# Taking the norm boundary into the feed-forward part: four up tiles, chunk by chunk

## The chip, the cores and the metric

The kernel runs on one core of a Trainium2 chip. The time is that of one execution on the device, in microseconds (us); the median of the runs counts, and lower is better. Engines: TensorE (PE; its weight loads are PEld), VectorE (DVE), ScalarE (ACT), GpSimd (POOL) and SyncE (SP), which issues transfers.

## The reference, cut to what matters

One inference step of a two-layer decoder. Each layer has a mixer (gated DeltaNet in the first, latent attention in the second) and a convolutional feed-forward part; each of the four is wrapped in two norms, and the sum is kept in x. Width 1024, feed-forward width 2816; 1040 prompt tokens and 8 sample tokens, 1048 in all. The change touches the place where the mixer's result is normed and added to x, x is normed for the feed-forward part, and its first up-projections begin.

```
def rmsnorm(x, w):
    xf = x.astype(jnp.float32)
    y = xf * lax.rsqrt(jnp.mean(xf * xf, axis=-1, keepdims=True) + NORM_EPS)
    return (y * w.astype(jnp.float32)).astype(x.dtype)

def conv_ffn(h, prev, w_up, conv_w, conv_b, w_down):
    u, new_prev = causal_dwconv(h @ w_up, prev, conv_w)
    gate, val = jnp.split(u + conv_b, 2, axis=-1)
    return (jax.nn.silu(gate) * val) @ w_down, new_prev

        x = x + rmsnorm(o, p['a_norm_post'][i])
...
        o, fconv = conv_ffn(rmsnorm(x, p['f_norm_pre'][layer]), ffn_conv0[layer],
                            p['f_w_up'][layer], p['f_conv_w'][layer], p['f_conv_b'][layer], p['f_w_down'][layer])
        x = x + rmsnorm(o, p['f_norm_post'][layer])
```

## The kernel before, in words

**Layout.** Features lie on the 128 partitions in 8 blocks, tokens along the free axis in three chunks (`CH`): chunk 0 with 280 tokens (the 8 samples, then 272 prompt tokens), chunks 1 and 2 with 384 each. The order of work is `ORD`, chunk 1, 2, 0. Every operand of a large product is split into a high half and the rest (`xh`, `xl` for activations, `wh`, `wl` for weights), and a product is three matmuls (`mm3`, L226 to L229): wh by xh (L227), wh by xl (L228), wl by xh (L229). A tile of up-projection over one chunk (`proj`) is 8 blocks of three, 24 matmuls.

**Weights.** `wprep` loads a 128-column tile, folds the norm's gain into it on GpSimd (L144), copies the high half on ScalarE (L151) and subtracts the low half on VectorE (L152).

**Output projection** (`outp`). It fills `acc` chunk by chunk in the order of `ORD`, 8 blocks each, through the two "mm" buffers of PSUM (`psop`); VectorE adds the result to `acc` (L336). In the first layer the last part of it has two heads (six matmuls for a block of a chunk), in the second layer four heads (twelve).

**Boundary** (`boundary`, one chunk). ScalarE squares `acc` in four pairs of blocks, VectorE adds them up (L259), two matmuls with ones make the statistic (`st_ps`, L265, issued at high priority; one row of a view counts each as two), ScalarE takes ln and exp (L106, L107). Then for each pair of blocks the old x is loaded (`xr`), `acc` is scaled (L285) and the residual added (L287, twice a pair). Then the high half on ScalarE (L293), its squares, their sum on VectorE (L259), the low half on GpSimd (L295), and a second statistic, whose result goes to `RS`. The up-projection reads `xh` and `xl` unscaled; `RS` is multiplied in when its result leaves PSUM.

**What calls it.** `boundaries` opens pools of its own, two statistic buffers in PSUM ("st") among them, runs the boundary for the three chunks, and closes them. Only then `ffn` opens its pools: the buffers for the products g (`fg`, four each of "gh" and "gl"), u and y (`fu`), down weights (`fdw`), and in PSUM "dn" (four) and "tr" (two).

**Feed-forward** (`ffn`). First six batches of stored convolution rows are loaded (`fsrow`, in the y buffers), transposed by TensorE into "tr" (`fpst`, L945, 44 transposes in all) and copied to `fstT` (L946). Then 11 groups of two pairs; a pair is one gate and one value tile, 24 matmuls for each chunk through the "mm" buffers. VectorE takes the result out of PSUM into `u` (L963, L964 for chunk 0, L966 for the others). `up_end` makes the convolution: ScalarE the first tap (L973), VectorE the other two (L975, over all 1064 columns, so all three chunks of the tile have to be there). Then silu, product (L999), high half and low half of g (L1004, L1007). The first pair alone goes chunk by chunk: both tiles on chunk 1, both on chunk 2, both on chunk 0. Every later tile takes its chunks in the order 0, 1, 2. From the second group on `down` of the group before comes in (`fdn`, in "dn").

**Order on the engines.** Nothing is put in order by hand at this place. A scheduler ranks the instructions by their order in the code and by buffers coming free, with the statistic's matmuls raised by `high_priority(2000)`, so each engine's order is not the order of the code.

## Time and profile before

| | us |
|---|---|
| median of 3 runs | 3313.66 |
| lowest, highest | 3309.49, 3319.81 |
| profiled execution | 3314.68 |
| its span | 3312.9 |

The mean granted clock of TensorE was 0.975 in the profiled execution. The part of it that the change touches lies at two places: from about 846 to 960 us (boundary of the first layer's mixer and the first up tiles) and from about 2455 to 2570 us (the same in the second layer). The views name instructions by line, engine and the program's names; "x4" counts instructions, and a number behind "<-" in brackets is idle time with what ended it. In the second layer the normed chunks have the names xbh and xbl, in the first xfh and xfl.

### The profile page before, as it was taken

The numbers are of one execution on the slowest core, as the hardware profiler recorded it, in microseconds if no ns is written. First come the engines' busy times: TensorE is split into PE (matmuls) and PEld (weight loads), VectorE is DVE, ScalarE is ACT, GpSimd is POOL, SyncE is SP. The second block draws the span as 40 slices with busy tenths as digits, with TensorE's granted clock in tenths as the row PEclk, the third lists the DMA queues.
The fourth block names the chain that finished last, engine by engine and source line by source line (L and its number), as shares of the span: only waits on it lengthen the run. The fifth ranks groups of instructions, "written<-read, shape, count | busy, mean of one in ns | idle before, by whom it ended". The sixth has DMA issues, their size and how long they took to land.

```text
span 3312.9 us, 52527 instructions
## 1 busy us (share of the span) xinstructions
PE 3123.5 (94%) x20846; PEld 2884.2 (87%) x20846; DVE 2030.3 (61%) x4139; ACT 1254.9 (38%) x2541; POOL 862.2 (26%) x1013
## 2 busy tenths in 40 slices
PE   7999999999899999999978999999998999999997
PEld 6888888888799999999967888856678999999996
DVE  4777777766864555555576676544557355555556
ACT  4656555563433222222334444433224322222223
POOL 1433222210342222322342111111105332322322
PEclk9999999999899999999989999999998999999999
DMA  3222222235321111111121000354432111111111
GB/s 107 62 65 69 64 67 59 72 105 176 96 66 46 39 52 49 48 46 39 45 86 44 25 27 28 108 189 184 159 102 84 46 46 45 46 45 52 46 39 66
DMA packets 267650, 235.08 MB, mean 71 GB/s; under 512 B 57919, under 2 KB 246597, under 8 KB 263285
## 3 DMA queue, kind: packets, MB, share of 16 engines
q1 hardware_dynamic: 260224, 189.69, 19.7%
q0 software_dynamic: 6912, 41.95, 3.4%
q8 instruction: 164, 2.69, 0.3%
q14 instruction: 82, 0.66, 0.1%
q10 hardware_dynamic: 268, 0.09, 0.0%
HBM read 198.84 MB, written 33.40 MB: 70 GB/s over the span
## 4 chain that ended last, share of the span: by engine, by line
PE 76%; DVE 14%; DMA 3%; issue 3%; ACT 2%; POOL 1%; SPq 0%; ACTq 0%; POOLq 0%; DVEq 0%
PE fps L228 9%; PE fps L229 9%; PE fps L227 9%; PE fdn L228 5%; PE fdn L227 5%; PE fdn L229 5%; PE psu L227 2%; PE psu L229 2%; PE po L1408 2%; PE psu L228 2%; PE dscr L1493 2%; DVE acc L287 2%; PE psop L227 1%; DVE tm L658 1%; DVE xs L660 1%
## 5 line engine op out<-in xcount | busy, mean ns | idle before, releaser
L144 POOL TENSOR_TENSOR ws<-ws,vec 128x1024 f32<-128x1024 f32 (+1 forms) x127 | 249.5, 1965 | 424.3 <-DMA ws<-in_f_w_up_dram 210.1
L228 PE MATMUL fps<-xfl,wh 128*128 128x384 f32 (+1 forms) x1056 | 343.7, 326 | 8.2 <-POOL xfl L295 8.1
L227 PE MATMUL fps<-xfh,wh 128*128 128x384 f32 (+1 forms) x1056 | 341.8, 324 | 8.0 <-ACT xfh L293 7.0
L228 PE MATMUL fps<-xbl,wh 128*128 128x384 f32 (+1 forms) x1056 | 343.6, 325 | 4.8 <-POOL xbl L295 4.7
L227 PE MATMUL fps<-xbh,wh 128*128 128x384 f32 (+1 forms) x1056 | 341.6, 324 | 1.1 <-ACT xbh L293 0.5
L229 PE MATMUL fps<-xfh,wl 128*128 128x384 f32 (+1 forms) x1056 | 342.4, 324 | 0.0
L229 PE MATMUL fps<-xbh,wl 128*128 128x384 f32 (+1 forms) x1056 | 341.2, 323 | 0.0
L966 DVE TENSOR_TENSOR fu<-fps,RS 128x384 f32<-128x384 f32 x176 | 98.0, 557 | 386.6 <-PE fps L229 386.1
L151 ACT CAST wh<-ws 128x1024 fp32r<-128x1024 f32 (+1 forms) x144 | 148.0, 1027 | 491.6 <-PE fps L228 373.8
L227 PE MATMUL fdn<-gh,dh 128*128 128x384 f32 (+1 forms) x960 | 315.2, 328 | 0.0
L228 PE MATMUL fdn<-gl,dh 128*128 128x384 f32 (+1 forms) x960 | 311.6, 325 | 0.0
L229 PE MATMUL fdn<-gh,dl 128*128 128x384 f32 (+1 forms) x960 | 308.6, 321 | 0.0
L1044 DVE TENSOR_TENSOR acc<-acc,fdn 128x384 f32<-128x384 f32 (+1 forms) x432 | 216.7, 514 | 108.8 <-PE fdn L229 108.0
L227 PE MATMUL psu<-xah,wh 128*128 128x384 f32 (+1 forms) x768 | 261.8, 341 | 9.5 <-ACT u L533 5.1
L228 PE MATMUL psu<-xal,wh 128*128 128x384 f32 (+1 forms) x768 | 260.0, 339 | 0.7 <-DVE xal L223 0.7
L229 PE MATMUL psu<-xah,wl 128*128 128x384 f32 (+1 forms) x768 | 259.0, 337 | 0.7 <-DVE wl L152 0.7
L975 DVE SCALAR_TENSOR_TENSOR fy<-fu,fcv,fy 128x1064 f32<-128x1064 f32 x176 | 238.6, 1357 | 7.6 <-ACT fy L973 7.3
L152 DVE TENSOR_TENSOR wl<-ws,wh 128x1024 fp32r<-128x1024 f32 (+1 forms) x144 | 173.6, 1206 | 71.3 <-ACT wh L151 71.1
L228 PEld LDWEIGHTS fps<-xfl,wh 128*128 128x128 f32 x1056 | 200.7, 190 | 10.8 <-POOL xfl L295 10.5
L227 PEld LDWEIGHTS fps<-xfh,wh 128*128 128x128 f32 x1056 | 200.3, 190 | 9.4 <-ACT xfh L293 7.9
L228 PEld LDWEIGHTS fps<-xbl,wh 128*128 128x128 f32 x1056 | 200.5, 190 | 6.9 <-POOL xbl L295 6.5
L227 PEld LDWEIGHTS fps<-xbh,wh 128*128 128x128 f32 x1056 | 200.2, 190 | 1.7 <-ACT xbh L293 0.9
(963 smaller groups left out, 7856.1 us busy)
## 6 DMA issues: line engine op xcount, KB each, us to landing
ws<-in_f_w_up_dram SPq DMA_DIRECT2D x88, 512.0 KB
ds<-in_f_w_down_dram SPq DMA_DIRECT2D x44, 512.0 KB
ws<-in_a_w_in_dram SPq DMA_DIRECT2D x32, 512.0 KB
xt<-in_x_prompt_dram SPq DMA_DIRECT2D x16, 512.0 KB
of<-og_d SPq DMA_DIRECT2D x32, 192.0 KB
xr<-x_d SPq DMA_DIRECT2D x16, 384.0 KB
GC<-gcd SPq DMA_DIRECT2D x24, 174.0 KB
Ss<-in_state_delta_S_dram SPq DMA_DIRECT2D x8, 512.0 KB
```

The costliest lines, as they stand in the source:

```text
L144: G.tensor_tensor(st, st, bc(fo, [P, kt, m]), op=ALU.mult)
L151: A.copy(hi, st)
L152: V.tensor_tensor(lo, st, hi, op=ALU.subtract)
L227: PE.matmul(ps, wh, ah, start=start, stop=False)
L228: PE.matmul(ps, wh, al, start=False, stop=False)
L229: PE.matmul(ps, wl, ah, start=False, stop=stop)
L287: V.scalar_tensor_tensor(a_[:, k + j, :], a_[:, k + j, :], vc(wname, k + j), res[j], op0=ALU.mult, op1=ALU.add)
L966: V.tensor_tensor(u[:, 18 + t0:18 + t0 + n], ps[:, :n], RS[:, t0:t0 + n], op=ALU.mult)
L975: V.scalar_tensor_tensor(y, u[:, j:j + LW], fcv[:, l, j, tl:tl + 1], y, op0=ALU.mult, op1=ALU.add)
L1044: V.tensor_tensor(acc[c][:, m, :], acc[c][:, m, :], ps[:, :n], op=ALU.add)
L1408: PE.matmul(po[:, :nq], vt[:kk, kb, P * (h % 2):P * (h % 2) + P], pT[:kk, j, :nq], start=(kb == 0), stop=(kb == i))
L1493: PE.matmul(sc[32 * j:32 * j + 32, :], ql[:, k, b, :], cT[:, j, :], start=(k == 0), stop=False, tile_position=(0, 32 * j))
```

## The change

`boundaries` is gone. `ffn` gets the name of the norm as an argument, and a new function `up_first` runs, for each chunk of `ORD`, its boundary and then four up tiles (the two pairs of the first group) on that chunk. What changes with it:

- The results of these four tiles go to the four "dn" buffers of PSUM (`up_mm(..., first=True)`), no longer to the two "mm" buffers.
- Gate and value tile of the second pair get their weight halves in the down weights' buffers ("dh", "dl") and their `u` in a "gh" and a "gl" buffer, which are made 1066 columns wide for that.
- The boundary's statistic goes to the "tr" buffers, which the transposes of the stored rows use as well; its sums go to the y buffers, its squares to "gl" (four, before two of its own); the old x goes by turns to the down weights' staging buffer and to two "u" tiles (before: two buffers of its own).
- The stored rows are loaded into "gh" instead of the y buffers. Their code stands ahead of the first boundary now.

```diff
--- before.py
+++ after.py
@@ -898,29 +898,9 @@
     es.close()
     xh, xl = open_x("xf")
 
-    def boundaries(wname):
-        with ExitStack() as es:
-            bp = es.enter_context(tc.tile_pool(name="bnd", bufs=1, reuse_waits="tile"))
-            xp = es.enter_context(tc.tile_pool(name="bxr", bufs=2, reuse_waits="tile"))
-            stp = es.enter_context(tc.tile_pool(name="bst", bufs=2, space=PSUM, reuse_waits="tile"))
-
-            def wide(nm):
-                if nm == "xr":
-                    return [xp.tile([P, 768], F32, tag=nm, name=nm)]
-                return bp.tile([P, 768], F32, tag=nm, name=nm, bufs=1 if nm[1].isdigit() else 2)
-
-            for c in ORD:
-                boundary(lambda nm: stp.tile([P, 512], F32, tag="st", name=nm), wide, c, wname, store=(c == 0))
-
-    boundaries("a_post")
...
-    def ffn(l, last):
+
+
+    def ffn(l, last, before):
         GR = 2
         NG = NFT // GR
         with ExitStack() as es:
@@ -938,26 +918,30 @@
             stT = fp.tile([P, 2 * NFT, 16], F32, name="fstT")
             for g in range(0, 2 * NFT, 8):
                 q = min(8, 2 * NFT - g)
-                srow = fup.tile([16, 8 * P], F32, tag=f"y{g // 8 % 2}", name="fsrow", bufs=1)
+                srow = gp.tile([16, 8 * P], F32, tag="gh", name="fsrow")
                 SP.dma_start(srow[:, :P * q], I["state_ffn_conv"][l, :, :, P * g:P * (g + q)].rearrange("s r c -> (s r) c"))
                 ps = stp.tile([P, 512], F32, tag="tr", name="fpst")
                 for j in range(q):
                     PE.transpose(ps[:, 16 * j:16 * j + 16], srow[:, P * j:P * j + P], ident[:16, :16])
                 V.tensor_copy(stT[:, g:g + q, :], ps[:, :16 * q].rearrange("p (a b) -> p a b", b=16))
             SP.dma_start(O["s_ffn_conv"][l, :, 0, :], I["state_ffn_conv"][l, :, 1, :])
-            def up_begin(tl):
+
+            def up_begin(tl, spare=None):
+
+                wx = iter("hl")
+                out = (lambda: dwp.tile([P, D], F32R, tag="d" + next(wx), name="wx")) if spare else None
                 wh, wl = wprep(wg, I["f_w_up"][l, :, P * tl:P * tl + P].rearrange("(k p) m -> p k m", p=P), KT, P,
-                               fold=f"f_pre{l}")
-                u = fup.tile([P, 26 + NP], F32, tag="u", name="fu")
+                               fold=f"f_pre{l}", out=out)
+                u = gp.tile([P, 26 + NP], F32, tag=spare, name="fu") if spare else fup.tile([P, 26 + NP], F32, tag="u", name="fu")
                 us = u[:, 0:24].rearrange("p (s r) -> p s r", r=3)
                 G.tensor_copy(us[:, :, 0:2], stT[:, tl, :].rearrange("p (s r) -> p s r", r=2))
                 G.memset(u[:, 24:26], 0.0)
                 return wh, wl, u, us
 
-            def up_mm(st, c):
+            def up_mm(st, c, first=False):
                 wh, wl, u, us = st
                 t0, n = CH[c]
-                ps = mtile("fps")
+                ps = dnp.tile([P, 384], F32, tag="dn", name="fps") if first else mtile("fps")
                 proj(ps[:, :n], wh, wl, c)
                 if c == 0:
                     V.tensor_tensor(us[:, :, 2], ps[:, 0:NS], RS[:, 0:NS], op=ALU.mult)
@@ -975,14 +959,21 @@
                     V.scalar_tensor_tensor(y, u[:, j:j + LW], fcv[:, l, j, tl:tl + 1], y, op0=ALU.mult, op1=ALU.add)
                 return y
 
-            def up_pair(i, cs, j, first=False):
-                if first:
-                    sg, sv = up_begin(i), up_begin(NFT + i)
-                    for c in ORD[:2]:
-                        for st in (sg, sv):
-                            up_mm(st, c)
-                    for st in (sg, sv):
-                        up_mm(st, ORD[2])
+            def up_first():
+
+                sts = []
+                for ci, c in enumerate(ORD):
+                    boundary(lambda nm: stp.tile([P, 512], F32, tag="tr", name=nm), wide_s, c, before, store=(c == 0))
+                    if ci == 0:
+                        for j in range(GR):
+                            sts += [up_begin(j, j and "gh"), up_begin(NFT + j, j and "gl")]
+                    for st in sts:
+                        up_mm(st, c, True)
+                return [(sts[2 * j], sts[2 * j + 1]) for j in range(GR)]
+
+            def up_pair(i, cs, j, st=None):
+                if st is not None:
+                    sg, sv = st
                 else:
                     sg = up_begin(i)
                     for c in range(3):
@@ -991,14 +982,14 @@
                 A.activation(yg, yg, AF.Silu)
                 if i == NFT - 1:
                     act_set()
-                if not first:
+                if st is None:
                     sv = up_begin(NFT + i)
                     for c in range(3):
                         up_mm(sv, c)
                 yv = up_end(sv, NFT + i, cs, GR + j)
                 V.tensor_tensor(yg, yg, yv, op=ALU.mult)
-                gh = gp.tile([P, T], F32R, tag="gh", name="gh")
-                gl = gp.tile([P, T], F32R, tag="gl", name="gl")
+                gh = gp.tile([P, 26 + NP], F32R, tag="gh", name="gh")[:, :T]
+                gl = gp.tile([P, 26 + NP], F32R, tag="gl", name="gl")[:, :T]
                 ysm = yg[:, 0:22:3]
                 A.copy(gh[:, 0:NS], ysm)
                 A.copy(gh[:, NS:], yg[:, 24:])
@@ -1053,10 +1044,16 @@
                     return [utile(nm), utile(nm)]
                 return fup.tile([P, LW], F32, tag="u", name=nm) if nm == "sq" else fup.tile([P, LW], F32, tag="y" + nm[1], name=nm, bufs=1)
 
+            def wide_s(nm):
+                if nm == "sq":
+                    return gp.tile([P, 26 + NP], F32, tag="gl", name=nm)
+                return wide_f(nm)
+
             prev = []
+            sts = up_first()
             for g in range(NG):
                 cs = sp.tile([P, 2 * GR, 10], F32, tag="cs", name="fcs")
-                parts = [up_pair(GR * g + j, cs, j, g + j == 0) for j in range(GR)]
+                parts = [up_pair(GR * g + j, cs, j, None if g else sts[j]) for j in range(GR)]
                 rows_out(g, cs)
                 end = g == NG - 1
                 if prev and not end:
@@ -1083,7 +1080,7 @@
                         else:
                             SP.dma_start(O["y_prompt"][0, 128 * (bi - 1):128 * bi, :], yt[:, :D])
 
-    ffn(0, False)
+    ffn(0, False, "a_post")
...
@@ -1616,13 +1613,7 @@
...
     xh, xl = open_x("xb", ORD)
-    boundaries("b_post")
...
-    ffn(1, True)
+    ffn(1, True, "b_post")
     xs_["es"].close()
     xs_["acc"].close()
 
```

With the same code for each operation, lines move: the transposes L945 are L925 after, the evictions L963, L964, L966 are L947, L948, L950, the convolution L975 is L959, the product L999 is L990, the down weight's split L1030 is L1021, the fold of weights stays L144, the state copies to u L953 are L937.

TensorE, second layer, around the statistic of the first chunk to be normed (s0 is its sum of squares, psop the output projection). Before:

```order
L228 MATMUL psop_24964<-ogl_24929,wx_24406 128x384
L229 MATMUL psop_24964<-ogh_24928,wx_24407 128x384
L227 MATMUL psop_24964<-ogh_24934,wx_24412 128x384
L228 MATMUL psop_24964<-ogl_24935,wx_24412 128x384
L265 MATMUL st_ps_25237<-s0_25226,ones_73 128x384 x2
L229 MATMUL psop_24964<-ogh_24934,wx_24413 128x384
L227 MATMUL psop_24964<-ogh_24940,wx_24418 128x384
L228 MATMUL psop_24964<-ogl_24941,wx_24418 128x384
```

After:

```order
L229 MATMUL psop_25184<-ogh_25082,wx_24425 128x272
L925 MATMUL fpst_25240<-ident_71,fsrow_25238 128x16 x8
L925 MATMUL fpst_25252<-ident_71,fsrow_25250 128x16 x8
L925 MATMUL fpst_25264<-ident_71,fsrow_25262 128x16 x8
L925 MATMUL fpst_25276<-ident_71,fsrow_25274 128x16 x8
L925 MATMUL fpst_25288<-ident_71,fsrow_25286 128x16 x8
L925 MATMUL fpst_25300<-ident_71,fsrow_25298 128x16
L265 MATMUL st_ps_25319<-s0_25308,ones_73 128x384 x2
L925 MATMUL fpst_25300<-ident_71,fsrow_25298 128x16 x3
L227 MATMUL fps_25412<-xbh1_25210,wh_25375 128x384
L227 MATMUL fps_25438<-xbh1_25210,wh_25385 128x384
```

The statistic stood inside a group of the output projection's matmuls on chunk 2; now it stands behind the last of them and behind 41 transposes.

VectorE, first layer, around the end of the first up tiles. Before (fu_10610 and fu_10620 are the u of the first pair, fu_10808 that of the third tile):

```order
L152 TENSOR_TENSOR wl_10805<-ws_10801,wh_10804 128x1024
L963 TENSOR_TENSOR fu_10610<-fps_10727,RS_85 128x8
L964 TENSOR_TENSOR fu_10610<-fps_10727,RS_85 128x272
L963 TENSOR_TENSOR fu_10620<-fps_10754,RS_85 128x8
L964 TENSOR_TENSOR fu_10620<-fps_10754,RS_85 128x272
L975 SCALAR_TENSOR_TENSOR fy_10783<-fu_10610,fcv_87,fy_10783 128x1064
L975 SCALAR_TENSOR_TENSOR fy_10790<-fu_10620,fcv_87,fy_10790 128x1064
L975 SCALAR_TENSOR_TENSOR fy_10783<-fu_10610,fcv_87,fy_10783 128x1064
L975 SCALAR_TENSOR_TENSOR fy_10790<-fu_10620,fcv_87,fy_10790 128x1064
L963 TENSOR_TENSOR fu_10808<-fps_10811,RS_85 128x8
L964 TENSOR_TENSOR fu_10808<-fps_10811,RS_85 128x272
```

After (fu_10508 is the u of the fourth tile, fu_11028 that of the fifth):

```order
L947 TENSOR_TENSOR fu_10508<-fps_10931,RS_85 128x8
L948 TENSOR_TENSOR fu_10508<-fps_10931,RS_85 128x272
L1021 TENSOR_TENSOR dl_11011<-ds_11008,dh_11010 128x1024
L152 TENSOR_TENSOR wl_11121<-ws_11117,wh_11120 128x1024
L959 SCALAR_TENSOR_TENSOR fy_10988<-fu_10508,fcv_87,fy_10988 128x1064
L959 SCALAR_TENSOR_TENSOR fy_10981<-fu_10498,fcv_87,fy_10981 128x1064
L959 SCALAR_TENSOR_TENSOR fy_10988<-fu_10508,fcv_87,fy_10988 128x1064
L959 SCALAR_TENSOR_TENSOR fy_10981<-fu_10498,fcv_87,fy_10981 128x1064
L1021 TENSOR_TENSOR dl_11017<-ds_11014,dh_11016 128x1024
L947 TENSOR_TENSOR fu_11028<-fps_11031,RS_85 128x8
L990 TENSOR_TENSOR fy_10981<-fy_10981,fy_10988 128x1064
```

Before, the evictions of two tiles ended there and one pair's convolution followed; now the fourth tile's eviction ends there, and the second pair's convolution and three weight splits stand between it and the fifth tile's first eviction.

GpSimd, first layer, between the low halves of the chunks (xfl1, xfl2, xfl0). Before:

```order
L954 MEMSET fu_10620 128x2
L144 TENSOR_TENSOR ws_10801<-ws_10801,vec_86 128x1024
L295 TENSOR_TENSOR xfl1_10314<-acc1_8619,xfh1_10313 128x768 x4
L953 COPY fu_10620<-fstT_10532 128x8x2
L295 TENSOR_TENSOR xfl2_10312<-acc2_8620,xfh2_10311 128x768 x4
L971 COPY fcs_10602<-fu_10610 128x2
L971 COPY fcs_10602<-fu_10620 128x2
L295 TENSOR_TENSOR xfl0_10310<-acc0_8618,xfh0_10309 128x560 x4
```

After:

```order
L937 COPY fu_10488<-fstT_10336 128x8x2
L144 TENSOR_TENSOR ws_10491<-ws_10491,vec_86 128x1024
L295 TENSOR_TENSOR xfl1_10314<-acc1_8619,xfh1_10313 128x768 x3
L937 COPY fu_10508<-fstT_10336 128x8x2
L938 MEMSET fu_10508 128x2
L295 TENSOR_TENSOR xfl1_10314<-acc1_8619,xfh1_10313 128x768
L144 TENSOR_TENSOR ws_10501<-ws_10501,vec_86 128x1024
L144 TENSOR_TENSOR ws_11021<-ws_11021,vec_86 128x1024
L295 TENSOR_TENSOR xfl2_10312<-acc2_8620,xfh2_10311 128x768 x4
```

The fold of the third tile's weights (ws_10801) stood ahead of chunk 1's low halves; now that of the third (ws_10491) stands ahead of them, and those of the fourth and fifth (ws_10501, ws_11021) between chunk 1's and chunk 2's.

## Rows read from the trace of the kernel before

**Rows 1.** The profile page, first part: busy time, share of the span, instructions:
```profile
PE 3123.5 (94%) x20846; PEld 2884.2 (87%) x20846; DVE 2030.3 (61%) x4139; ACT 1254.9 (38%) x2541; POOL 862.2 (26%) x1013
```

**Rows 2.** Table by stretch: us, each engine's busy time (count), clock, DMA, GB/s:
```profile
1000.00:1040.00 40.00, 40.00 (x256) 40.00 (x255) 11.33 (x14) 16.04 (x29) 9.42 (x11) 1.00 0.18 53
```

**Rows 3.** The same table: boundary and first two up tiles of either part:
```profile
866.80:926.00 59.20, 43.31 (x196) 35.70 (x195) 50.16 (x59) 27.71 (x42) 29.77 (x17) 0.80 0.26 77
2487.30:2534.00 46.70, 38.03 (x194) 34.36 (x194) 37.21 (x44) 22.09 (x33) 26.46 (x18) 0.82 0.35 111
```

**Rows 4.** Whom TensorE waited for, 866.8 to 926: us in total, times, longest:
```profile
PE fps L228 <- POOL xfl L295: 8.1, 5, 3.2
PE fps L227 <- ACT xfh L293: 7.0, 3, 3.5
```

**Rows 5.** The same, 2487.3 to 2534:
```profile
PE fps L228 <- POOL xbl L295: 4.7, 4, 1.5
PE fpst L945 <- DVE fstT L946: 3.3, 1, 3.3
```

**Rows 6.** VectorE in order of time, first part: start, us, line, operation [idle before]:
```profile
853.76 0.95 DVE L285 TENSOR_TENSOR acc<-acc,st_r 128x768 f32<-128x768 f32 x1
...
880.32 0.94 DVE L259 TENSOR_TENSOR s<-s,sq 128x768 f32<-128x768 f32 x1
...
887.13 1.82 DVE L285 TENSOR_TENSOR acc<-acc,st_r 128x768 f32<-128x768 f32 x2 [2.15 <-ACT st_r L107]
...
908.94 1.39 DVE L285 TENSOR_TENSOR acc<-acc,st_r 128x560 f32<-128x560 f32 x2
...
924.26 0.16 DVE L963 TENSOR_TENSOR fu<-fps,RS 128x8 f32<-128x8 f32 x1
...
957.08 0.43 DVE L964 TENSOR_TENSOR fu<-fps,RS 128x272 f32<-128x272 f32 x1
```

**Rows 7.** The same view, two runs of chunk 2:
```profile
888.87 2.20 DVE L287 SCALAR_TENSOR_TENSOR acc<-acc,vec,xr 128x384 f32<-128x384 f32 x4
...
897.97 8.33 DVE L259 TENSOR_TENSOR s<-s,sq 128x768 f32<-128x768 f32 x6
```

**Rows 8.** One line, 830 to 940: ns min/median/max, first and last start:
```profile
L295 POOL TENSOR_TENSOR xfl<-acc,xfh x12: 1388/2336/3517, 868.2 to 919.2; 128x768 fp32r<-128x768 f32 x8, 128x560 fp32r<-128x560 f32 x4
```

**Rows 9.** TensorE in order of time, first part:
```profile
846.61 0.85 PE L945 MATMUL fpst<-ident,fsrow 16*128 16x16 f32 x11
...
850.47 1.45 PE L265 MATMUL st_ps<-s,ones 128*128 128x384 f32 x4
```

**Rows 10.** Groups by line, shape, VectorE 838 to 980: busy, mean ns, idle:
```profile
L975 DVE SCALAR_TENSOR_TENSOR fy<-fu,fcv,fy 128x1064 f32<-128x1064 f32 x12 | 17.6, 1488 | 3.2 <-ACT fy L973 3.1
...
L152 DVE TENSOR_TENSOR wl<-ws,wh 128x1024 fp32r<-128x1024 f32 x8 | 9.8, 1222 | 4.6 <-ACT wh L151 4.6
...
L966 DVE TENSOR_TENSOR fu<-fps,RS 128x384 f32<-128x384 f32 x12 | 6.7, 556 | 17.6 <-PE fps L229 17.0 <-ACT RS L107 0.5
```

**Rows 11.** The same, GpSimd:
```profile
L144 POOL TENSOR_TENSOR ws<-ws,vec 128x1024 f32<-128x1024 f32 x8 | 15.6, 1946 | 55.9 <-DVE acc L336 38.4 <-DMA ws<-in_f_w_up_dram 17.5
```

**Rows 12.** TensorE in order of time, second part:
```profile
2457.14 1.56 PE L265 MATMUL st_ps<-s,ones 128*128 128x384 f32 x4 [0.43 <-DVE s L259]
...
2474.56 1.56 PE L265 MATMUL st_ps<-s,ones 128*128 128x384 f32 x4
...
2487.27 1.16 PE L945 MATMUL fpst<-ident,fsrow 16*128 16x16 f32 x16
```

**Rows 13.** VectorE in order of time, second part:
```profile
2459.91 0.96 DVE L285 TENSOR_TENSOR acc<-acc,st_r 128x768 f32<-128x768 f32 x1 [2.00 <-ACT st_r L107]
...
2531.48 0.17 DVE L963 TENSOR_TENSOR fu<-fps,RS 128x8 f32<-128x8 f32 x1 [1.61 <-ACT RS L107]
...
2564.96 0.43 DVE L964 TENSOR_TENSOR fu<-fps,RS 128x272 f32<-128x272 f32 x1
```

**Rows 14.** The chain that ended last, a later boundary: start, us, what:
```profile
1711.83 2.68 DMA xr<-x_d
```

10 lines of the change are left out of this document (removed).

## Prediction

> **What bounds the kernel now.** I read the page's first part first: TensorE is busy for 94% of the span and its weight loads for 87% [rows 1]. In the steady feed-forward 256 matmuls take 40.0 us, none idle [rows 2]. 24 matmuls over a chunk are thus 24 x 40/256 = 3.75 us on the mean of the three chunks; by columns (384, 384, 280) that is 4.1, 4.1 and 3.0 us, and an up tile is 11.3 us. So the change can only win or lose where TensorE stops or runs slowly: at the boundaries. Next the table by stretch. From the last output-projection matmul to the end of the first pair of up tiles TensorE is busy 43.3 of 59.2 us at a mean granted clock of 0.80 in the first feed-forward part, and 38.0 of 46.7 us at 0.82 in the second [rows 3]. The reader is to see two losses: idle time (15.9 and 8.7 us) and a clock that falls to the half level. Third, who TensorE waits for there: GpSimd's low halves and ScalarE's high halves of the normed chunk, 15.1 us in the first part [rows 4]; in the second 4.7 us for the low halves and 3.3 us for a copy of state rows [rows 5]. These are ends of one chain, which the order of time on VectorE shows [rows 6]: statistic, scale (L285), residual (L287), split, squares, next chunk's statistic. VectorE is busy 50.2 of 59.2 us there [rows 3], so behind TensorE's waits it is nearly full.
>
> **Two facts on that chain.** VectorE and GpSimd wait for each other. Six adds of squares (L259) take 8.33 us where GpSimd works, while four L287, with GpSimd at rest, take 2.20 us, 0.55 each [rows 7]. GpSimd's subtraction takes 1.39 us at its shortest and 2.34 us at its median [rows 8]; 2.34 is 1.39 plus one add of 0.95. I therefore add the operations of both engines up, one after the other. The Trainium skill (SBUF - State Buffer, Who interferes with whom) speaks against this change in the same way: a VectorE instruction with two SBUF inputs and a GpSimd instruction that reads SBUF exclude each other for the whole instruction. By that rule no matmul put between makes the chain shorter, and each weight fold moved between makes it longer; if the engines did not exclude each other, the sums below would fall by GpSimd's share, some 6 us per chunk. The rows decide for the first.
>
> **First part, step by step.** (1) The six state batches now use the two "tr" PSUM buffers that the statistic of the boundary uses as well, and they come ahead of it. On TensorE the statistic moves behind three more groups of six output-projection matmuls (3 x 1.0 us) and 31 more transposes (0.85/11 us each, 2.4 us) [rows 9]: from 850.5 to 856.0, and L285 from 853.8 to 859.3. VectorE's backlog of evictions is smaller by then, so part of it comes back: up to the end of chunk 2's squares there are 4 L285 (0.95), 8 L287 (0.55), 8 evictions (about 0.45), 6 adds (0.95), a weight split (1.22 [rows 10]) and 4 subtractions on GpSimd (1.39), 24.3 us, so 883.6 where it was 881.3 [rows 6]. The statistic's way to L285 is 3.3 us (850.5 to 853.8), and the fourth tile's split and the second tile's eviction now stand ahead of L285: about 890, where it was 887.1. (2) Chunk 2 took 21.8 us to the next L285 [rows 6]; one more eviction (0.56 [rows 10]) and one fold (1.95 [rows 11]) stand in it: 24.3 us, 914.3 instead of 908.9. (3) From there to the first tile's last eviction 15.3 us; two evictions and most of a 24-matmul run more, since the statistic now stands early in tile 1: 17.7 us, 932 instead of 924.3. (4) Now VectorE has the convolution of four tiles in one piece: 8 L959 (1.49, with what contention they had) 11.9 us, 4 splits 4.9, 2 products 2.5, evictions 2.4, some 1.3 us for ScalarE and the folds: 23 us, to 955.0. TensorE meanwhile does tiles 2 to 4 of chunk 0, two chunks of tile 5 and 12 down matmuls, and would be through at 932 + 9.0 + 0.5 + 7.1 + 2.1 = 950.7; the third chunk of tile 5 needs one of two "mm" buffers, whose eviction stands at the end of that backlog. Before, that eviction ended at 957.5 [rows 6]. So 2.5 us are won there, and the 12 down matmuls (2.1 us) are done already: **-4.6 us**. Of the 15.9 us idle and the slow clock little is won, because the wait moves from the boundary to the buffers.
>
> **Second part.** (5) Here the same sharing of "tr" costs much more. Before, the statistic of chunk 1 ran at 2457.1, 30 us ahead of the last output-projection matmul (2487.3) [rows 12], and three statistics ran under those matmuls. Now it stands behind all of them. Three statistics of 1.1 us and a wait of 0.4 us leave the stream, so it ends at 2483.5; then 44 transposes (3.4 us) through two buffers, with a 1.2 us split between VectorE's copies: statistic at 2488, L285 at 2490.8 instead of 2459.9 [rows 13]. TensorE has nothing to do meanwhile. (6) Chunk 1 up to the next L285: 4 L285, 8 L287, 6 adds, a split, 4 subtractions, a fold: 3.8 + 4.4 + 5.7 + 1.2 + 5.6 + 1.95 = 22.7, plus 3.3 for the statistic and 0.6 for an eviction: 2517.3. (7) Chunk 2 by the first part's row, 21.8 and some: 22, 2539.3. (8) Chunk 0 to tile 1's last eviction 18.2 (here 24 matmuls follow the statistic): 2557.5. (9) The same backlog, 23: 2580.5. Before, that eviction ended at 2565.4 [rows 13]. Loss 15.1, less 2.1 for the down matmuls: **+13.0 us**.
>
> **Edits costed at nothing.** The residual loads use a down-weight buffer and two "u" buffers in place of a pool of two. A load is asked for when the pair two ahead is done, as before, some 3.4 us ahead of its use (two L287, two L285); with that cover gone it costs what a like load cost in chunk 0 of the later boundary, 2.68 us on the chain [rows 14]. The down weights load later; their first use lies 15 us behind. Squares get four buffers for two; I take nothing for it, since in chunk 0 the six adds run in one piece [rows 7], so that no add waits for a buffer there.
>
> **Sum.** 13.0 - 4.6 = 8.4 us more than the profiled execution's 3314.68: 3323.1. That execution lies 1.0 us over the median, so 3322. Bounds: the backlog (4, 9) is 17 us if it hides under TensorE as far as its own operations allow, 27 if ScalarE and GpSimd add in full; the chunk sums move by 6 us each if GpSimd's share were free or its median of 2.34 counted. That gives 0 to -12 for the first part and +5 to +22 for the second.
>
> **Rivals.** *TensorE sets the stage (same or faster).* If the backlog is under the 18.7 us that TensorE has in hand (950.7 - 932), step 4 gives -6.8 - 2.1 = -9, step 9 gives +8: 3313. For it: before, VectorE sat idle for stretches here. Against: 20 us of its own operations. *The clock.* The four tiles keep TensorE busier; were the granted clock at 1.00 instead of 0.80 and 0.82, at most 0.20 x 59.2 + 0.18 x 46.7 = 20 us of matmul time would come back, and if that were what ends the stage, 3314 + 8 - 20 = 3302. The Trainium skill (TensorE: Matmul & The Clock Gate, HAM oscillation) says that a loop that keeps matmuls together holds the high clock. The trace agrees that the clock falls after pauses, but the matmuls wait in these stages for the chain on VectorE, whose speed the clock does not touch; hence a small chance. *Loads in borrowed buffers (slower).* With six chunks and 2.68 us for each, 16 us more: 3338. It decides as soon as the stretch from asking to using falls under the load's time; in chunk 0 (280 columns) it is 2.9 us, so it may strike twice.
>
> **How the numbers follow.** My sum 0.50 (3314 to 3330, its middle at the line of 0.3%, 9.9 us, which is about what a measurement tells from no change); TensorE sets the stage 0.22 (3304 to 3316); the clock 0.10 (below 3304); loads 0.18 (3328 to 3340). Faster by over 0.3%: 0.11. Within: the second and about half of the first, 0.47. Slower: 0.42. The range that leaves out some 2 in 10: 3304 to 3338.
>
> **What would show it.** In the second part the statistic at about 2488 and TensorE idle for some 6 us behind it; L285 of chunks 1, 2, 0 near 2491, 2517, 2539; behind tile 4 TensorE waiting for VectorE's eviction for 4 us or more in both parts; GpSimd folds between the subtractions. Wrong if TensorE does not wait behind tile 4, if L285 of the second part starts before 2480, or if VectorE waits for residual loads.

## The result, and the profile after

The changed kernel is **slower: 3336.08 us** (median of 6 runs, 3331.30 to 3345.49) against 3318.15 for the kernel before in the same runs; the ratio is 1.0063, 95% interval 1.0039 to 1.0087, so 21 us (13 to 29); the two medians lie 17.9 us apart. Of all kernels below, the ratio is the measure of time. One run each of e_dn, e_dn_xr and e_place5 was far longer than the others (5981, 7595 and 4336 us) and stands in no ratio. The profiled execution of the changed kernel took 3345.49 us, some 9 above its median, so sums of stages are compared here, not whole spans.

Part one of the page of the changed kernel (busy time, share, instructions) says little, as [rows 1] did: TensorE has 15 us more, VectorE 14.

```profile
PE 3138.7 (94%) x20846; PEld 2897.8 (87%) x20846; DVE 2044.3 (61%) x4139; ACT 1253.7 (37%) x2541; POOL 871.0 (26%) x1013
```

**Where the time went.** Two stages carry the change. Each is taken from the start of the last output-projection matmul (psop) to the start of the state rows (frow) of the eleventh group, and all the steady work of a part lies in it too, which is the same in all kernels. Such a stage repeats well: with unchanged code the first took 753.9 and 752.9 us in two kernels, the second 741.7 and 742.3; with the changed code 753.0 and 752.7, 768.0 and 768.6. The widest such pair is the second stage of before_low_v and e_mix, 733.6 and 736.4. So differences under 3 us are not read from one trace.

| kernel | first stage, us | second stage, us | ratio to before, 95% interval |
|---|---|---|---|
| before | 753.9 | 741.7 | |
| changed | 753.0 | 768.0 | 1.0063 (1.0039 to 1.0087) |
| e_first_only | 752.7 | 742.3 | 1.0004 (0.9988 to 1.0019) |
| e_second_only | 752.9 | 768.6 | 1.0060 (1.0041 to 1.0079) |
| e_two | 755.0 | 766.5 | 1.0073 (1.0053 to 1.0093) |
| e_dn | 754.9 | 756.6 | 1.0048 (1.0031 to 1.0065) |
| e_dn_xr | 755.1 | 754.5 | 1.0037 (1.0020 to 1.0055) |
| e_place | 745.0 | 752.9 | 1.0017 (1.0003 to 1.0031) |
| e_place5 | 747.8 | 753.3 | 1.0026 (1.0011 to 1.0041) |
| e_place_late | 747.3 | 751.7 | 1.0000 (0.9984 to 1.0015) |
| e_low_v | 744.4 | 751.5 | 0.9994 (0.9980 to 1.0008) |
| before_low_v | 749.1 | 733.6 | 0.9965 (0.9949 to 0.9981) |
| e_place_low_v | 736.6 | 745.4 | 0.9939 (0.9916 to 0.9961) |
| e_mix | 736.7 | 736.4 | 0.9920 (0.9895 to 0.9944) |

The changed kernel won 0.9 us in the first stage and lost 26.3 in the second. The output projection ahead of the second became some 2.7 us shorter (means of four kernels each, 339.6 with the old order and 336.9 with the new, single traces up to 3.5 us around that), which fits that the statistics left it.

**The second stage after.** VectorE in order of time (start, us, line, operation, idle before), to be read against [rows 13]: scale of chunks 1, 2 and 0, the first tile's last eviction, two instructions of the backlog, the fifth tile's first eviction.

```profile
2498.88 2.48 DVE L285 TENSOR_TENSOR acc<-acc,st_r 128x768 f32<-128x768 f32 x2 [1.10 <-ACT st_r L107]
...
2527.15 1.83 DVE L285 TENSOR_TENSOR acc<-acc,st_r 128x768 f32<-128x768 f32 x2 [0.67 <-ACT st_r L107]
...
2550.65 1.39 DVE L285 TENSOR_TENSOR acc<-acc,st_r 128x560 f32<-128x560 f32 x2 [1.10 <-ACT st_r L107]
...
2570.43 0.17 DVE L947 TENSOR_TENSOR fu<-fps,RS 128x8 f32<-128x8 f32 x1 [2.92 <-PE fps L229]
...
2582.78 3.49 DVE L152 TENSOR_TENSOR wl<-ws,wh 128x1024 fp32r<-128x1024 f32 x1
...
2592.38 2.86 DVE L990 TENSOR_TENSOR fy<-fy 128x1064 f32<-128x1064 f32 x1
2595.16 0.43 DVE L948 TENSOR_TENSOR fu<-fps,RS 128x272 f32<-128x272 f32 x1
```

GpSimd beside those two instructions of the backlog, a low half of g and a fold:

```profile
2582.54 2.65 POOL L998 TENSOR_TENSOR gl<-fy,gh 128x1040 fp32r<-128x1040 f32 x1 [0.75 <-ACT gh L995]
...
2590.28 3.83 POOL L144 TENSOR_TENSOR ws<-ws,vec 128x1024 f32<-128x1024 f32 x1 [5.09 <-DMA ws<-in_f_w_up_dram]
```

TensorE in order of time there: the end of the output projection is at 2491.0, then the transposes, the statistic, the wait for the first high half; later the wait behind tile 4, and where the slow matmuls behind it end. This answers to [rows 12].

```profile
2490.95 2.21 PE L925 MATMUL fpst<-ident,fsrow 16*128 16x16 f32 x32
...
2494.96 2.12 PE L265 MATMUL st_ps<-s,ones 128*128 128x384 f32 x4 [0.32 <-DVE fstT L926]
...
2503.33 1.01 PE L227 MATMUL fps<-xbh,wh 128*128 128x384 f32 x2 [5.82 <-ACT xbh L293]
...
2595.73 0.66 PE L227 MATMUL fps<-xbh,wh 128*128 128x384 f32 x1 [4.81 <-DVE fu L948]
2596.19 0.53 PE L228 MATMUL fps<-xbl,wh 128*128 128x384 f32 x1
2596.51 0.53 PE L229 MATMUL fps<-xbh,wl 128*128 128x384 f32 x1
...
2601.31 0.49 PE L229 MATMUL fps<-xbh,wl 128*128 128x384 f32 x1
2601.63 0.34 PE L227 MATMUL fps<-xbh,wh 128*128 128x384 f32 x1
2601.81 0.34 PE L228 MATMUL fps<-xbl,wh 128*128 128x384 f32 x1
```

Whom TensorE waited for from 2486 to 2600 (us in total, times, longest), to be read against [rows 5]: the low halves' share doubled, the wait for the statistic is new, and the waits for the high half and for the fifth tile's eviction were 0.5 us each before.

```profile
PE fps L228 <- POOL xbl L295: 9.6, 5, 3.7
PE fps L227 <- ACT xbh L293: 5.8, 1, 5.8
PE fps L227 <- DVE fu L948: 4.8, 1, 4.8
PE st_ps L265 <- DVE s L259: 3.7, 1, 3.7
```

The table by stretch, from the end of the output projection to the fifth tile's first eviction, and from there to the third group's state rows; first the changed kernel, then the one before.

```profile
2490.70:2595.60 104.90, 78.68 (x423) 69.50 (x421) 86.33 (x93) 44.29 (x61) 50.89 (x39) 0.85 0.28 85
2595.60:2704.20 108.60, 108.41 (x665) 107.92 (x666) 43.92 (x55) 36.83 (x52) 35.31 (x43) 0.97 0.15 44
```
```profile
2487.10:2565.40 78.30, 67.63 (x380) 63.17 (x380) 59.55 (x66) 34.27 (x46) 41.97 (x36) 0.89 0.28 88
2565.40:2673.60 108.20, 108.15 (x680) 107.66 (x679) 44.02 (x55) 37.06 (x52) 36.77 (x44) 1.00 0.15 45
```

The first stretch is 26.6 us longer, and 15.6 of that is idle time of TensorE (26.2 for 10.7). VectorE's busy time grew by 26.8 (93 instructions for 66; those of chunk 1 and part of chunk 2 had run under the output projection), as much as the stretch. That fits a chain through VectorE that sets the pace; experiments 4 and 9 test it.

**The first stage after**, VectorE in order of time, to be read against [rows 6]. The changed kernel's output projection began 6.1 us later in its execution (722.6 for 716.5), ahead of all that the change touches; less these 6.1 the five starts are 859.5, 890.4, 914.9, 931.9 and 956.6.

```profile
865.59 0.96 DVE L285 TENSOR_TENSOR acc<-acc,st_r 128x768 f32<-128x768 f32 x1
...
896.50 1.83 DVE L285 TENSOR_TENSOR acc<-acc,st_r 128x768 f32<-128x768 f32 x2 [0.50 <-ACT st_r L107]
...
920.98 1.39 DVE L285 TENSOR_TENSOR acc<-acc,st_r 128x560 f32<-128x560 f32 x2 [1.09 <-ACT st_r L107]
...
937.95 0.17 DVE L947 TENSOR_TENSOR fu<-fps,RS 128x8 f32<-128x8 f32 x1 [3.23 <-PE fps L229]
...
962.67 0.43 DVE L948 TENSOR_TENSOR fu<-fps,RS 128x272 f32<-128x272 f32 x1
```

TensorE behind tile 4 in this stage: the same wait, and where the slow matmuls behind it end.

```profile
963.24 0.66 PE L227 MATMUL fps<-xfh,wh 128*128 128x384 f32 x1 [4.81 <-DVE fu L948]
...
966.26 0.52 PE L227 MATMUL fps<-xfh,wh 128*128 128x384 f32 x1
...
966.79 0.34 PE L229 MATMUL fps<-xfh,wl 128*128 128x384 f32 x1
```

### The profile page after: what moved, and what is told of

The parts are those of the page before. It is cut to its first block, busy times and chain, and to the rows that moved or that the text cites. A ratio compares the mean times of both kernels' runs of the same rounds, so it can differ in the third digit from the quotient of the medians.

```text
span 3343.7 us, 52515 instructions
## 1 busy us (share of the span) xinstructions
PE 3138.7 (94%) x20846; PEld 2897.8 (87%) x20846; DVE 2044.3 (61%) x4139; ACT 1253.7 (37%) x2541; POOL 871.0 (26%) x1013
## 4 chain that ended last, share of the span: by engine, by line
PE 76%; DVE 14%; DMA 3%; issue 3%; ACT 2%; POOL 1%; SPq 0%; DVEq 0%; ACTq 0%; POOLq 0%
PE fps L228 9%; PE fps L227 9%; PE fps L229 9%; PE fdn L228 5%; PE fdn L229 5%; PE fdn L227 5%; PE psu L227 2%; PE psu L229 2%; PE psu L228 2%; PE po L1405 2%; PE dscr L1490 2%; DVE acc L287 2%; PE psop L227 1%; PE psop L229 1%; PE psop L228 1%
## 5 line engine op out<-in xcount | busy, mean ns | idle before, releaser
L144 POOL TENSOR_TENSOR ws<-ws,vec 128x1024 f32<-128x1024 f32 (+1 forms) x127 | 252.9, 1992 | 405.1 <-DMA ws<-in_f_w_up_dram 169.3
L227 PE MATMUL fps<-xbh,wh 128*128 128x384 f32 (+1 forms) x1008 | 327.7, 326 | 10.8 <-ACT xbh L293 5.8
L228 PE MATMUL fps<-xbl,wh 128*128 128x384 f32 (+1 forms) x1008 | 328.4, 326 | 9.6 <-POOL xbl L295 9.6
L228 PE MATMUL fps<-xfl,wh 128*128 128x384 f32 (+1 forms) x1008 | 327.2, 325 | 10.3 <-POOL xfl L295 10.3
L950 DVE TENSOR_TENSOR fu<-fps,RS 128x384 f32<-128x384 f32 x176 | 98.0, 557 | 387.7 <-PE fps L229 381.1
L227 PE MATMUL fps<-xfh,wh 128*128 128x384 f32 (+1 forms) x1008 | 327.4, 325 | 6.7 <-DVE fu L948 4.8
L229 PE MATMUL fps<-xbh,wl 128*128 128x384 f32 (+1 forms) x1008 | 327.7, 325 | 0.0
L229 PE MATMUL fps<-xfh,wl 128*128 128x384 f32 (+1 forms) x1008 | 326.0, 324 | 0.0
L151 ACT CAST wh<-ws 128x1024 fp32r<-128x1024 f32 x140 | 143.7, 1027 | 475.2 <-PE fps L228 370.3
L959 DVE SCALAR_TENSOR_TENSOR fy<-fu,fcv,fy 128x1064 f32<-128x1064 f32 x176 | 235.9, 1343 | 3.1 <-ACT fy L957 2.7
L152 DVE TENSOR_TENSOR wl<-ws,wh 128x1024 fp32r<-128x1024 f32 x140 | 173.3, 1238 | 66.4 <-ACT wh L151 66.1
L228 PEld LDWEIGHTS fps<-xbl,wh 128*128 128x128 f32 x1008 | 192.1, 191 | 12.4 <-POOL xbl L295 12.1
L228 PEld LDWEIGHTS fps<-xfl,wh 128*128 128x128 f32 x1008 | 191.2, 190 | 13.0 <-POOL xfl L295 12.7
L227 PEld LDWEIGHTS fps<-xfh,wh 128*128 128x128 f32 x1008 | 191.1, 190 | 8.5 <-issue 5.1
```

Source lines behind the costliest of these rows:

```text
L144: G.tensor_tensor(st, st, bc(fo, [P, kt, m]), op=ALU.mult)
L151: A.copy(hi, st)
L152: V.tensor_tensor(lo, st, hi, op=ALU.subtract)
L227: PE.matmul(ps, wh, ah, start=start, stop=False)
L228: PE.matmul(ps, wh, al, start=False, stop=False)
L229: PE.matmul(ps, wl, ah, start=False, stop=stop)
```

## The experiments

**1 and 2. One part alone.** The functions `boundaries` and `ffn` of before stand beside the new `ffn`, and each part uses one of them.

```diff
 e_first_only
-    ffn(1, True, "b_post")
+    boundaries("b_post")
+    ffn_old(1, True)
 e_second_only
-    ffn(0, False, "a_post")
+    boundaries("a_post")
+    ffn_old(0, False)
```

> The first feed-forward part as in the changed kernel, the second as before. Theory (the loss sits in the second part, where the statistic moved behind the whole output projection): from the first output-projection matmul of the first part to the state rows of its third group the changed kernel took 348.0 us where before took 349.2, so the kernel is 0 to 2 us faster than before. Rival (what costs is the four tiles and their backlog of convolutions, alike in both parts): half of the loss of 21 us, 10 us slower than before.

> The first part as before, the second as in the changed kernel. Theory: 22 to 24 us slower than before, the whole loss; from the first output-projection matmul to the first eviction of the fifth tile 440.8 us as in the changed kernel, against 417.4. Rival (alike in both parts): 10 us slower.

Measured 1.0004 and 1.0060; in e_second_only the fifth tile's first eviction ended 439.1 us after the start of the output projection (440.8 in the changed kernel, 417.4 before). The whole loss is the second part's, and the parts don't touch each other. "Alike in both parts" falls.

**3. Two tiles, not four.**

```diff
-                        for j in range(GR):
-                            sts += [up_begin(j, j and "gh"), up_begin(NFT + j, j and "gl")]
+                        sts += [up_begin(0), up_begin(NFT)]
...
-                return [(sts[2 * j], sts[2 * j + 1]) for j in range(GR)]
+                return [(sts[0], sts[1]), None]
```

> The changed kernel with two up tiles in each chunk's stretch, not four; the second pair follows as every later one. Theory (the four tiles are a gain, the place of the statistic the loss): the first tile's last eviction comes some 3 us earlier, but from there to the fifth tile's first eviction it is 32.8 us as before, not 24.6: 5 us slower than the changed kernel in each part, some 30 us slower than before. Rival (four tiles with their backlog are the loss): 5 to 10 us slower than before.

Both were wrong: 1.0073, 24 us, with stages of 755.0 and 766.5. Against the changed kernel that is 2.0 us more and 1.5 less. From the first tile's eviction to the fifth tile's it was 33.6 us in the second part, about as I had expected, but the first tile's came 8.9 us earlier after the start of the output projection (407.3 for 416.2), not 3: fewer evictions, and TensorE through sooner. So four tiles in place of two are worth nothing either way that these runs can show, and the loss is in what both kernels share: the boundary's new place and its borrowed buffers.

**4. The statistic gets the "tr" buffers alone.**

```diff
-                ps = stp.tile([P, 512], F32, tag="tr", name="fpst")
+                ps = dnp.tile([P, 384], F32, tag="dn", name="fpst")
```

> The changed kernel, but the stored rows are transposed into the four dn buffers, so the statistic has the two tr buffers alone. Theory (the shared buffers hold the statistic back): in the second part the first statistic runs some 30 us before the output projection ends; the statistic's wait of 4.2 us, its way to the scale of 3.9 us, four scales (3.8 us) and half of the residual adds (2.2 us) leave the chain behind the output projection, 14 us in all: 7 us slower than before instead of 21. The other half of the residuals is loaded into the down weights' staging buffer, which the order places behind the output projection. Rival (the buffers don't matter, what costs is the longer chain and the backlog of four tiles): 21 us slower as in the changed kernel.

Measured 1.0048, 16 us, where the theory had 7 and the rival 21. The second stage fell by 11.4 of the 14, but its output projection took 339.5 us (336.0 in the changed kernel), with a statistic in it again, and the first stage 1.9 us more. TensorE and VectorE in order of time in this kernel: chunk 1's statistic and scale are back under the output projection (which ends at 2495), but the statistic of the normed chunk 1 and that of chunk 2, the 2513.22 and 2517.81 ones, still stand behind it.

```profile
2467.82 1.56 PE L265 MATMUL st_ps<-s,ones 128*128 128x384 f32 x4 [0.38 <-DVE s L259]
...
2513.22 1.45 PE L265 MATMUL st_ps<-s,ones 128*128 128x384 f32 x4
...
2517.81 1.56 PE L265 MATMUL st_ps<-s,ones 128*128 128x384 f32 x4 [1.58 <-DVE s L259]
```
```profile
2470.58 0.96 DVE L285 TENSOR_TENSOR acc<-acc,st_r 128x768 f32<-128x768 f32 x1 [2.01 <-ACT st_r L107]
```

**5. And the first chunk's old x in "u" tiles of the outer pool.**

```diff
                     nxr[0] += 1
-                    if nxr[0] % 2:
+                    if nxr[0] % 2 and nxr[0] > 4:
```
(with the edit of 4)

> As the one before, and the old x of the first chunk goes to u tiles alone, not by turns to the down weights' staging buffer. Theory (borrowed buffers lie where the output projection still works): the whole residual, the split and the second statistic of chunk 1 run under the output projection too: four residual adds (2.2 us), four low halves (5.6 us) and three adds (2.9 us) leave the chain, some 10 us more, so 3 us faster than before to 3 us slower. Rival (only the statistic mattered): as the one before, 7 us slower.

Measured 1.0037, 12 us, where I expected none: the second stage fell by 2.1 us only. Chunk 1 is now done under the output projection (its second statistic at 2485.4, the projection's end at 2490.0), and chunk 2's scale comes 18.7 us behind the start of the last output-projection matmul, where it was 26.2 in 4. But of these 7.5 us 4.2 are left at chunk 0's scale and 2.0 at the first tile's eviction. On the way chunk 2's sums of squares begin 6.2 us behind the projection's end, and TensorE waits for sums of this chunk at two statistics, for 5.3 and 5.5 us.

```profile
2508.39 0.96 DVE L285 TENSOR_TENSOR acc<-acc,st_r 128x768 f32<-128x768 f32 x1 [3.09 <-ACT st_r L107]
```

**6. Other places for the borrowed buffers.** Three edits beside that of 4: the pool of u and y is opened first, so that it lies where the boundary's own pools lay; the squares use its two "u" buffers and the old x only "u" tiles of the outer pool; all four first tiles have their `u` in "gh" and "gl".

```diff
+            fup = pool("fu", 2)
             gp = pool("fg", 2 * GR)
             fp = pool("fconst", 1)
-            fup = pool("fu", 2)
...
-                if nm == "sq":
-                    return gp.tile([P, 26 + NP], F32, tag="gl", name=nm)
+                if nm == "xr":
+                    return [utile(nm), utile(nm)]
                 return wide_f(nm)
```

> The changed kernel with other places for the borrowed buffers: the stored rows are transposed into dn, the boundary's sums and squares use the u and y buffers and these are opened first (where the boundary's own pools lay before), the old x goes to u tiles of the outer pool, and all four first tiles have their u in gh and gl. Theory (the loss of the second part is that the boundary's buffers are taken by or lie under work that ends with the output projection): three statistics run under the output projection again; the scale of chunk 0 comes some 27 us behind its end as before (25.8) and two evictions more, the first tile's last eviction at 46, the fifth tile's first at 71, the third group's rows at 249 where before had 256, so 5 to 8 us faster than before. Rival (chain on VectorE and GpSimd behind the output projection as long as with the two edits before): rows at 269, 12 us slower.

Measured 1.0017, 5.6 us slower: between the two. All three statistics run under the output projection again, as foretold, and the first stage gained 8 us, which I had not foretold: from the first tile's last eviction to the fifth tile's first it is 13.2 us there, where the changed kernel had 25.2, and 6 us of that are lost again up to the third group's rows. The three edits were made together, so which of them did this is not shown. But in the second stage the rows (they are those of the fourth group, not the third as the expectation calls them) come at 267, not 249. Chunk 2's scale in that stage of this kernel, whom TensorE waited for, and the first of these waits in order of time:

```profile
2483.89 2.42 DVE L285 TENSOR_TENSOR acc<-acc,st_r 128x768 f32<-128x768 f32 x2
```

```profile
PE st_ps L265 <- DVE s L259: 12.2, 2, 9.6
PE fps L227 <- DVE fu L948: 4.8, 1, 4.8
```
```profile
2511.10 2.93 PE L265 MATMUL st_ps<-s,ones 128*128 128x384 f32 x4 [9.57 <-DVE s L259]
```

A new wait took the place of the old: the second statistic of chunk 2, raised in priority, was put 38 matmuls ahead of the end of chunk 1's four tiles, and while it waits for VectorE those matmuls wait behind it.

**7. That statistic without its raised priority.**

```diff
-            with tc.high_priority(2000):
+            with ExitStack() if late else tc.high_priority(2000):
...
-        finish(sm, RS[:, t0:t0 + n])
+        finish(sm, RS[:, t0:t0 + n], late)
```
(late for chunk 2 of this boundary, on top of 6)

> The kernel with the buffers in other places, and the second statistic of chunk 2 without its raised priority: in the second part it stands behind all four tiles of chunk 1 instead of 38 matmuls ahead of their end; the first part's order is unchanged. Theory (what was left of the second part's loss is TensorE's wait of 9.6 us at a statistic that stands ahead of ready matmuls): 38 matmuls, 6.6 us, move into the wait: 1 us faster than before to 1 slower, where the other was 5.6 slower. Rival (the chain sets the end, not the order on TensorE): still 5 to 6 us slower.

Measured 1.0000 (0.9984 to 1.0015), 5.6 us better than 6 by the ratios, though the intervals overlap. In the profile TensorE's idle time at statistics fell from 12.2 to 7.5 us, the second stage from 752.9 to 751.7, and the first stage became 2.3 us longer; both differences are under the 3 us that one trace can tell. So the order on TensorE may be part of the second stage's loss, but this pair does not show it, and the rest of the loss stays open.

```profile
PE st_ps L265 <- DVE s L259: 7.5, 3, 3.1
```

**8. More buffers for the fifth tile.** On top of 6 its three results go to "dn" too.

```diff
                     for c in range(3):
-                        up_mm(sg, c)
+                        up_mm(sg, c, i == GR)
```

> The kernel before this one, and the fifth tile's results go to the four dn buffers as well. Theory (behind tile 4 TensorE waits for a buffer whose eviction stands behind VectorE's backlog): the wait of 4.8 us and some 2 us of slow clock behind it go in both parts, 13 us in all: 18 to 21 us faster than before. Rival (the backlog is only met one tile later): as the kernel before this one.

The rival was right: 1.0026, no faster than 6. TensorE passes tile 5 and then waits in the same way, in the first part ahead of tile 7 and in the second ahead of the third chunk of tile 6:

```profile
PE fps L227 <- DVE fu L950: 3.4, 1, 3.4
```
```profile
PE fps L227 <- DVE fu L948: 3.2, 1, 3.2
```

More buffers move the wait to a later tile; they don't take it away.

**9. The low halves on VectorE**, in the changed kernel.

```diff
-            G.tensor_tensor(xl[c][:, k:k + 2, :], a_[:, k:k + 2, :], xh[c][:, k:k + 2, :], op=ALU.subtract)
+            (low or G).tensor_tensor(xl[c][:, k:k + 2, :], a_[:, k:k + 2, :], xh[c][:, k:k + 2, :], op=ALU.subtract)
```

> The changed kernel, but the boundary ahead of the feed-forward tiles subtracts its low halves on VectorE, not GpSimd (12 in each part). Theory (VectorE and GpSimd shut each other out, so their times add up): each subtraction costs the chain 0.95 us in place of 1.39 at least, 1.8 us a chunk less, 9 us in the two parts: 12 us slower than before where the changed kernel is 21 slower. Rival (GpSimd works beside VectorE): VectorE has 3.8 us a chunk more, 20 us in the two parts: some 40 us slower than before.

Measured 0.9994: 23 us faster than the changed kernel, where the theory had 9 and the rival the other sign. VectorE got 12 instructions more in each part, and the stages became 8.6 and 16.5 us shorter. One line's durations (ns, shortest, median, longest) in the second part, low halves (L295) and adds of squares (L259), first in the changed kernel, then in this one:

```profile
L295 POOL TENSOR_TENSOR xbl<-acc,xbh x12: 1641/2381/4650, 2503.4 to 2561.8; 128x768 fp32r<-128x768 f32 x8, 128x560 fp32r<-128x560 f32 x4
...
L259 DVE TENSOR_TENSOR s<-s,sq x15: 736/1715/2656, 2511.5 to 2562.6; 128x768 f32<-128x768 f32 x9, 128x560 f32<-128x560 f32 x6
```
```profile
L295 DVE TENSOR_TENSOR xbl<-acc,xbh x12: 731/948/959, 2500.6 to 2551.3; 128x768 fp32r<-128x768 f32 x8, 128x560 fp32r<-128x560 f32 x4
...
L259 DVE TENSOR_TENSOR s<-s,sq x15: 733/947/959, 2503.6 to 2550.7; 128x768 f32<-128x768 f32 x9, 128x560 f32<-128x560 f32 x6
```

From the last output-projection matmul to the end of the first tile's last eviction it takes 67.8 us in this kernel and 80.2 in the changed one. 12.4 us over 12 subtractions is 1.03 each, on top of the 0.88 that one takes on VectorE (eight of 0.95, four of 0.73): by this estimate a subtraction on GpSimd cost the chain some 1.9 us, not 1.39. In the first part the same stretch gives 9.4 us, so 1.7 for each. The Trainium skill (SBUF — State Buffer, Who interferes with whom) says that a VectorE instruction with two inputs in SBUF and a GpSimd instruction that reads SBUF shut each other out, and that the order of issue decides who waits. The trace agrees with the first: the adds fall from a median of 1.72 us to 0.95 as soon as the subtractions leave GpSimd. No run here shows the second.

**10. The same in the kernel before.**

> The kernel before, with the low halves of these two boundaries on VectorE. Theory (GpSimd's and VectorE's times add up, a subtraction costs the chain some 0.85 us more on GpSimd): the first part gains as the changed kernel did, some 9 us; in the second part the chunks 1 and 2 are done under the output projection, so only chunk 0's four and what chunk 2 drags behind the projection count, 3 to 5 us: 12 to 14 us faster than before. Rival (only the changed kernel's fuller chain made GpSimd dear): no difference from before.

Measured 0.9965, 12 us: the theory's sum, though split otherwise, 4.8 us in the first stage and 8.1 in the second. So the price of GpSimd was there before the change; the change put more of it on the path. With the low halves on VectorE in both kernels the change costs 10 us (0.9994 against 0.9965; 3 to 17 by the intervals) in place of 21, and by the stages 13.2 in place of 25.4: about half of its cost hung on GpSimd's low halves.

**11. Both edits, 6 and 9.**

> The kernel with the buffers in other places, and the low halves on VectorE. Theory (two causes, which add up: what the second part's chain lost to the projection's end, and GpSimd on the chain): first part 8 us shorter than with either alone, second part without the 9.6 us wait of the statistic of chunk 2, since the order now has it 37 matmuls later: 15 to 20 us faster than before. Rival (both edits free the same wait): as the better of the two, 2 us faster than before.

Measured 0.9939, 20 us faster than before, the theory's sum, though not its second half. In the first stage the gains add up (736.6; 745.0 and 744.4 with either alone). In the second, 745.4, it stays 3.7 over before: a statistic ahead of ready matmuls still stops TensorE for 5.9 us in one piece, which the theory had foretold to go, and tile 5 waits as in the changed kernel. Against the kernel of 10, which has the low halves on VectorE as well (733.6), the new scheme still costs 11.8 us in this stage with both of these causes taken out; what these 11.8 us are made of was not tested.

```profile
PE st_ps L265 <- DVE s L259: 5.9, 1, 5.9
PE fps L227 <- DVE fu L948: 4.8, 1, 4.8
```

**12. The better half of each**: the first part of 11, the second part of 10.

> First part: the changed scheme with the buffers in other places and the low halves on VectorE; second part: the scheme of before with the low halves on VectorE. Theory (the parts are independent): from the last output-projection matmul to the last group's state rows 736.6 us in the first part (before 753.9) and 733.6 in the second (before 741.7): 25 us faster than before. Rival (a faster first part is given back in the second): as the better of the two kernels it is made of, 20 us faster.

Measured **0.9920 (0.9895 to 0.9944), 3292.15 us median**, 27 us by the ratio; the stages of the profiled execution are 736.7 and 736.4, 22.5 us together less than before. It beats both kernels; the interval holds the theory's 25 us and the rival's 20, so it doesn't decide between them. Part one of its page:

```profile
PE 3119.8 (95%) x20846; PEld 2883.3 (88%) x20846; DVE 2022.5 (61%) x4163; ACT 1255.3 (38%) x2541; POOL 810.8 (25%) x989
```

## Why the prediction was wrong, step by step

The direction and the places were right; the size was not: 8.4 us forecast, 21 measured. No rival came about. TensorE does not set the stage behind tile 4 (it waits there for 4.8 us in both parts); the granted clock did not win anything (0.85 in the second part's stretch, 0.89 before); VectorE waited for no residual load, so that the measured 3336 lies in that rival's range (3328 to 3340) is chance.

**First part, -4.6 forecast, about -1 measured.** Steps 1 to 3 held within a microsecond: the scales were forecast at 859.3, 890 and 914.3 and the first tile's eviction at 932; they came at 859.5, 890.4, 914.9 and 931.9. Steps 2 and 3 were made of stretches of the trace between two events, with the contention inside. Step 1 was a sum of single instructions up to the second scale, with GpSimd's subtractions at their shortest; its terms give 888.7, and that "about 890" hit 890.4 is in part luck. Step 4, the backlog, was 23 us by the sum of single instructions and took 25.2. The rows of the second part, where it took as long, show it: the split L152 took 3.49 us, not 1.22, and the product L990 2.86, not 1.27, just where GpSimd has its own subtraction L998 and fold L144 (3.48 and 2.85 us in the first part). I had set "some 1.3 us for ScalarE and the folds" for all of that. The 12 down matmuls that were "done already" were worth 2.1 us in the sum and 0.7 in the trace (107.5 us from the fifth tile's first eviction to the third group's rows, 108.2 before), since TensorE starts at the half clock behind its wait of 4.8 us: 10 matmuls some 0.32 us apart and then 0.17, about 10 x 0.15 = 1.5 us.

**Second part, +13.0 forecast, +23 measured** (26.3 in the stage, less some 3 in the output projection). Step 5 was right: behind the end of the output projection the statistic was forecast at 4.5 us and the scale at 7.3, and they came at 3.9 and 7.9, with TensorE idle for 5.8 us. That the sharing of "tr" does this is shown by experiment 4. That it is not all that holds the chain back is shown by 6: with the buffers in other places chunk 2's scale comes 2.6 us behind the start of the last output-projection matmul, where it came 18.7 behind it in 5. Little of that reaches the stage, which fell by 1.6 us only (754.5 to 752.9). The forecasts of the steps behind it are each too short:

| step | forecast, us | measured, us |
|---|---|---|
| 6, scale of chunk 1 to that of chunk 2 | 26.5 | 28.3 |
| 7, to that of chunk 0 | 22.0 | 23.5 |
| 8, to the first tile's eviction | 18.2 | 19.8 |
| 9, backlog to the fifth tile's first eviction | 23.0 | 25.2 |
| 9, less the down matmuls | -2.1 | +0.4 |

In e_second_only, the same code in another trace, steps 6 to 9 took 27.6, 23.5, 19.8 and 25.2 us.

Step 6 took the subtractions at their shortest, 1.39 us, where the median of [rows 8] was 2.34; experiment 9 puts the price at some 1.9, which for four of them is 2.0 us more, as much as was missing. Step 7 took chunk 2's 21.8 us from the first part "and some", without the fold and the eviction that step 2 had added to the same row (24.3). In the trace neither came: no fold ran between these two scales, and three evictions as in the row. So the 1.5 us that were missing there are not traced to an instruction. Step 8 has the same contention; in the kernel of experiment 9 steps 6, 7 and 8 took 23.5, 22.1 and 13.7 us. Step 9 is the backlog of step 4 once more; that its excess is GpSimd's fold and low half of g is read from the rows, as no run moved these. The last line is the clock: from the fifth tile's first eviction to the third group's rows it was 108.6 us for 108.2, though 12 matmuls fewer lay in it. In the rows above, 18 matmuls start 0.32 us apart and then 0.17, which is 18 x 0.15 = 2.7 us: what the down matmuls gave, the slow clock took.

Some 14 us were missing in all, 3.7 in the first part and 10.3 in the second. The term that was mis-sized most is **the price of GpSimd beside VectorE**: 2.2 us in each backlog (steps 4 and 9), 1.8 in step 6 and, by experiment 9, probably the 1.6 of step 8. The second is the slow clock behind the wait at tile 5, which the sum had at nothing when it credited the 12 down matmuls in full: 1.4 and 2.5 us. Step 7's 1.5 us stay open. My bounds for each chunk sum (6 us either way) held the truth, but those for the second part, +5 to +22, missed its +23; the value in the sum was taken from the lower end, though the row's median lay at the other.

## What to carry to other kernels

When a stretch is bounded by a chain through two engines that hold each other up, price a moved step by the stretch of the trace that it comes from, contention inside, and not by the shortest time of its instructions; in the first part the two steps of this prediction that did so were right within 1 us, while the same rows carried over to the second part were 1.5 and 1.6 us short. Here a subtraction on GpSimd cost the chain more than on VectorE (some 1.9 us for 0.88): ask, whenever both work on the same chain, what the second engine's instruction costs the first. And a borrowed buffer can carry the order of its other users along, as the "tr" buffers did here: before a boundary borrows PSUM or SBUF from a later phase, see on TensorE's order whether its first matmul has slipped behind the work that used to hide it, as here behind 41 transposes.

## What the runs showed of the hardware that was not expected

- With 12 subtractions moved from GpSimd to VectorE, VectorE got faster: its adds fell from a median of 1.72 us to 0.95, and a stage with 12 more VectorE instructions became 16.5 us shorter.
- Behind a pause of 4.8 us, TensorE's granted clock was at the lower of its two levels for 18 matmuls in the second part (0.32 us apart, then 0.17), which cost 2.7 us more than the pause itself. Behind a pause of the same length in the first part it was so for 10 matmuls, some 1.5 us. So one such pause does not give the price of the next.
